# Activations of 32 of the 384 dense tokens from gathered rows of u

## The chip, the cores and the metric

The kernel runs on one core of a Trainium2 chip. The metric is the time of one execution on the device in microseconds, the median of several runs; lower is better. The core's engines run their own instruction streams in order: PE (matmul; its weight loads are listed apart as PEld), DVE (elementwise on vectors), ACT (activation functions and copies), POOL (here it only issues gathers), SP (it issues the plain DMAs). They wait for each other through semaphores.

## The reference

One transformer layer on 512 tokens of width 1024: a token-mixing part (sparse attention and a pooling mixer), and then a channel-mixing part, PEER: each token picks 128 of 16384 one-neuron experts.

```python
def peer_ffn(h, w_q, sub_keys, u, v):
    ...
        q = (hx @ w_q).reshape(TOKEN_BLOCK, PEER_HEADS, 2, PEER_HALF)
        s = jnp.einsum('nhpd,hpkd->nhpk', q, sub_keys).astype(jnp.float32)
        top_s, top_i = lax.top_k(s, PEER_TOPK)
        ...
        expert = (i1 * N_KEYS + i2).reshape(TOKEN_BLOCK, PEER_HEADS * PEER_TOPK)
        gate = jax.nn.softmax(best_s, axis=-1).reshape(TOKEN_BLOCK, PEER_HEADS * PEER_TOPK).astype(hx.dtype)
        u_sel = u[expert]
        v_sel = v[expert]
        act = jax.nn.gelu(jnp.einsum('nd,ned->ne', hx, u_sel), approximate=False)
        return jnp.einsum('ne,ned->nd', gate * act, v_sel)
```

u and v are tables of 16384 rows of 1024 float32 (4 KB a row, 64 MB a table). A token needs 128 rows of each.

## The kernel before

The token mixing takes the first part of the program and is not touched. The channel mixing treats the 512 tokens in two ways.

**Dense tokens** (384, `ND`): the activation of every one of the 16384 experts is computed for every dense token, whether the token picked it or not, and a gate matrix that is zero for all experts not picked removes the rest. The experts are cut into 128 chunks of 128. For a chunk, `fetch` loads 512 KB of the transposed u (tile `ue`), ACT rounds it to a float32r high part (`uhe`), DVE subtracts to get the low part (`ule`), and PE forms the product with h2 (also split in high and low) in 24 matmuls, 8 slices of k times 3 passes, each 384 columns wide, into a PSUM tile `pse`; ACT applies gelu. Later the chunk is multiplied by its gates (`gated`), split again (`weights`: `Wh`, `Wl` from the weights, `vh`, `vl` from 512 KB of v), and contracted with v in 18 matmuls of 512 columns (`contract`, tiles `acc`).

**Sparse tokens** (the last 128): `sparse` gathers the 128 picked rows of u, one for each of the 128 tokens in an indirect DMA (512 KB), and DVE takes the dot product of each row with the token's h2 (`hx`) in one instruction with an accumulator (line 756); then the same for v (line 767), where each row is scaled and added to `sacc`.

The program has two stages in the channel mixing. **The act stage**: PE computes the activations of the first chunks (`dense_acts`, 59 of them) while the product keys are selected (`ProductKeys`, on DVE) and the gate matrix is built (`gates`): DVE makes one-hot matrices (`on`, `oa`) for 4 tokens at a time, PE multiplies them (tiles `gm`), ACT copies the result to `st`, SP writes it to DRAM (`gd`). Of the 59 chunks 35 stay in SBUF (`KEPT = HOLD - 1`), the other 24 (`SPILL`) are written to DRAM (`ad`). How the two kinds of work interleave follows from `act_until` with the shares in `FILL`; outside the last stage the order on an engine is then made by a scheduler. **The last stage** goes through the 128 chunks in an order written by hand: in iteration c it prepares the weights of chunk c+1, multiplies chunk c+2 by its gates, issues some rows of `sparse` (`EARLY`, `RATE` or `late` rows for an iteration), for c < 24 reloads a spilled chunk, for the next 69 iterations computes the activations of one more chunk (`multiply`), and contracts chunk c. So there are 24 iterations with reloads, 69 with activations, and 35 (`KEPT`) with the contraction alone. The tiles `v`, `vh`, `vl`, `Wh`, `Wl` have two buffers, rows five, the gates of eight chunks (`g`) two.

Of the kernel before, what the change touches and what calls it, by code (L numbers as in the profile page):

```python
# [20 lines left out]
P = 128  # L21
# [13 lines left out]
ND = DENSE * P  # L35
NEXP = 128
GT = 16
GJ = 8
HOLD = 36
SPILL = 24  # L40
# [3 lines left out]
EARLY = 0.8  # L44
DELAY = 2.0
RATE = 3.0
# [6 lines left out]
FILL = (0.36, 0.72, 1.0)  # L53
# [11 lines left out]
K_ID, K_IOTA, K_BLK, K_RC, NCONST = 0, 128, 256, 384, 448  # L65
# [5 lines left out]
def layer(ctx, tc, xT, cvec, w_ada, cols, consts, w_in, w_grp, w_up, w_out, w_pq, subk, u, uT, v, out):  # L71
# [14 lines left out]
    ad = tc.dram_tile([SPILL, P, ND], F32, name="ad")  # L86
# [8 lines left out]
    with ExitStack() as pre:  # L95
# [405 lines left out]
        hx = k2.tile([P, D], F32, name="hx")  # L501
# [74 lines left out]
    def dense_acts(n):  # L576


        for c in range(n):
# [19 lines left out]
    with ExitStack() as win:  # L599
# [38 lines left out]

# [435 lines left out]
```

## Time and profile before

| | |
|---|---|
| time before, median of 3 runs | 1548.25 us (1547.19 to 1548.95) |
| the profiled execution | 1546.26 us, span of its instructions 1544.5 us |
| PE busy | 1501.2 us, 97% of the span, 8011 matmuls |
| PE weight loads | 1308.0 us, 85% |
| DVE busy | 1282.3 us, 83% |
| ACT busy | 650.7 us, 42% |
| POOL busy | 324.6 us, 21% |
| DMA | 394.69 MB, 256 GB/s over the span |

The act stage lies between about 397 and 725 us, the last stage between 725 and 1544 us. A matmul's busy time is counted from its start to its modelled end, and matmuls are pipelined, so that the next one starts well before that end: durations of matmuls must not be added; what PE can do is read from the distance between the starts of neighbouring matmuls. The same holds, by some 0.1 us, for DVE.

### The profile page before, as it was taken

Reading aid. Unit: us, or ns where it says so; the run is one execution under the profiler, and the core shown is the slowest. Engines: PE = TensorE matmul, PEld = TensorE weight load, DVE = VectorE, ACT = ScalarE, POOL = GpSimd, SP = SyncE. Lnnn points to the kernel's source line nnn. Section 1 sums busy time; section 2 is a strip of 40 time slices with the busy share of each in tenths; the row PEclk is TensorE's granted clock in tenths of the full one; section 3 lists DMA queues with packets and bytes.
Section 4 is the critical chain, followed back from the end, with each engine's and each line's share of the span. In section 5 each row is a group of like instructions: output and inputs, shape, how many; then the busy total and the mean of one; then the engine's idle time right before and its main releaser. Section 6 shows DMA issues by size and latency. Waiting matters only on the chain.

```text
span 1544.5 us, 22464 instructions
## 1 busy us (share of the span) xinstructions
PE 1501.2 (97%) x8011; PEld 1308.0 (85%) x8011; DVE 1282.3 (83%) x2632; ACT 650.7 (42%) x1005; POOL 324.6 (21%) x318
## 2 busy tenths in 40 slices
PE   5999999999999999999999999999999999999998
PEld 3678788877899989899878999999999999998886
DVE  8799886866898898983778888888888888888887
ACT  4643555642345454554333333333333333333332
POOL 0000000000000000001123444444444444453320
PEclk9999999999999999999999999999999999999999
DMA  8422664531135656789889999999998999998983
GB/s 317 159 83 75 232 229 144 190 140 55 50 125 182 204 178 200 219 258 332 305 311 361 349 324 362 318 356 340 338 357 320 359 325 353 352 334 308 329 305 144
DMA packets 159121, 394.69 MB, mean 256 GB/s; under 512 B 13601, under 2 KB 69025, under 8 KB 158882
## 3 DMA queue, kind: packets, MB, share of 16 engines
q1 hardware_dynamic: 122146, 259.04, 48.0%
q0 software_dynamic: 36864, 134.23, 24.6%
q8 instruction: 62, 1.02, 0.3%
q14 instruction: 49, 0.40, 0.1%
HBM read 359.14 MB, written 34.08 MB: 255 GB/s over the span
## 4 chain that ended last, share of the span: by engine, by line
PE 76%; DVE 15%; DMA 5%; ACT 3%; issue 2%; SPq 0%; ACTq 0%; DVEq 0%
PE acc L829 28%; PE pse L570 6%; PE pse L569 6%; PE pse L568 6%; PE pse L585 4%; PE pse L587 4%; PE pse L586 4%; DMA v<-v 3%; PE gm L687 2%; DVE bias L348 2%; DVE ule L548 1%; DVE m L347 1%; PE po L471 1%; PE pso L172 1%; PE pso L173 1%
## 5 line engine op out<-in xcount | busy, mean ns | idle before, releaser
L754 POOL DMA_INDIRECT ur<-u,ei x128 | 156.8, 1225 | 630.5 <-ACT Wh L818 383.7
L829 PE MATMUL acc<-vl,Wh 128*128 128x512 f32 x768 | 237.1, 389 | 0.7 <-DVE vl L821 0.5
L829 PE MATMUL acc<-vh,Wh 128*128 128x512 f32 x768 | 236.8, 389 | 0.6 <-ACT vh L819 0.6
L829 PE MATMUL acc<-vh,Wl 128*128 128x512 f32 x768 | 237.4, 390 | 0.0
L762 POOL DMA_INDIRECT vr<-v,ei x128 | 164.9, 1288 | 208.3 <-DVE sacc L767 178.2
L821 DVE TENSOR_TENSOR vl<-v,vh 128x1024 fp32r<-128x1024 f32 x128 | 156.9, 1225 | 60.1 <-ACT vh L819 59.7
L570 PE MATMUL pse<-h2h,ule 128*128 128x384 f32 x552 | 185.2, 336 | 0.4 <-DVE ule L548 0.4
L569 PE MATMUL pse<-h2l,uhe 128*128 128x384 f32 x552 | 184.7, 335 | 0.0
L568 PE MATMUL pse<-h2h,uhe 128*128 128x384 f32 x552 | 184.4, 334 | 0.0
L548 DVE TENSOR_TENSOR ule<-ue,uhe 128x1024 fp32r<-128x1024 f32 x128 | 156.0, 1218 | 26.3 <-ACT uhe L547 26.1
L818 ACT ACTIVATE Wh<-gelu 128x384 fp32r<-128x384 f32 x104 | 54.6, 525 | 281.6 <-PE acc L829 169.5
L829 PEld LDWEIGHTS acc<-vl,Wh 128*128 128x128 f32 x768 | 143.9, 188 | 31.5 <-DVE vl L821 1.7
L585 PE MATMUL pse<-h2h,uhe 128*128 128x384 f32 x472 | 169.1, 358 | 1.0 <-ACT uhe L547 0.8
L829 PEld LDWEIGHTS acc<-vh,Wl 128*128 128x128 f32 x768 | 144.2, 188 | 30.0
L767 DVE SCALAR_TENSOR_TENSOR sacc<-vr,wt,sacc 128x1024 f32<-128x1024 f32 x127 | 162.9, 1282 | 2.8 <-DMA vr<-v,ei 0.4
L829 PEld LDWEIGHTS acc<-vh,Wh 128*128 128x128 f32 x768 | 143.1, 188 | 25.5 <-ACT vh L819 1.0
L587 PE MATMUL pse<-h2h,ule 128*128 128x384 f32 x472 | 160.1, 339 | 3.2 <-DVE ule L548 3.1
L586 PE MATMUL pse<-h2l,uhe 128*128 128x384 f32 x472 | 159.5, 338 | 0.0
L547 ACT ACTIVATE uhe<-ue 128x1024 fp32r<-128x1024 f32 x128 | 134.3, 1049 | 55.2 <-PE pse L586 45.9
L756 DVE SCALAR_TENSOR_TENSOR ur<-ur,hx 128x1024 f32<-128x1024 f32 x128 | 150.6, 1220 | 0.0
L819 ACT ACTIVATE vh<-v 128x1024 fp32r<-128x1024 f32 x128 | 135.8, 1061 | 12.2 <-DMA v<-v 12.2
L569 PEld LDWEIGHTS pse<-h2l,uhe 128*128 128x128 f32 x552 | 103.6, 188 | 3.2
(430 smaller groups left out, 2674.6 us busy)
## 6 DMA issues: line engine op xcount, KB each, us to landing
ue<-uT SPq DMA_DIRECT2D x128, 512.0 KB, 5.3
v<-v SPq DMA_DIRECT2D x128, 512.0 KB, 5.8
wada<-w_ada SPq DMA_DIRECT2D x48, 512.0 KB, 4.4
gd<-st SPq DMA_DIRECT2D x24, 1024.0 KB, 5.7
g<-gd SPq DMA_DIRECT2D x48, 512.0 KB, 7.8
ad<-gelu SPq DMA_DIRECT2D x24, 192.0 KB, 3.2
wgp<-w_in SPq DMA_DIRECT2D x8, 512.0 KB, 3.2
wga<-w_in SPq DMA_DIRECT2D x8, 512.0 KB, 5.0
```

The costliest lines, as they stand in the source:

```text
L548: V.tensor_tensor(lo, src, hi.bitcast(F32), op=ALU.subtract)
L568: T.matmul(p, hi[:, k, :], h2h[:, k, :n], start=(k == 0), stop=False)
L569: T.matmul(p, hi[:, k, :], h2l[:, k, :n], start=False, stop=False)
L570: T.matmul(p, lo[:, k, :], h2h[:, k, :n], start=False, stop=(k == DT - 1))
L585: T.matmul(ps, hi[:, k, :], h2h[:, k, :ND], start=(k == 0), stop=False)
L586: T.matmul(ps, hi[:, k, :], h2l[:, k, :ND], start=False, stop=False)
L587: T.matmul(ps, lo[:, k, :], h2h[:, k, :ND], start=False, stop=(k == DT - 1))
L754: G.indirect_dma_start(out=ur, out_offset=None, in_=u, in_offset=bass.IndirectOffsetOnAxis(ap=ei3[:, k:k + 1], axis=0))
L762: G.indirect_dma_start(out=vr, out_offset=None, in_=v, in_offset=bass.IndirectOffsetOnAxis(ap=ei3[:, k:k + 1], axis=0))
L767: V.scalar_tensor_tensor(sacc, vr, wt[:, k:k + 1], sacc, op0=ALU.mult, op1=ALU.add)
L821: V.tensor_tensor(vl, vr, vh.bitcast(F32), op=ALU.subtract)
L829: T.matmul(acc[tb][i], x[:, t], y[:, i * 512:(i + 1) * 512], start=(c == 0 and n == 0), stop=(c == NEXP - 1 and n == 2))
```

## The change

32 of the dense tokens (the first ones, `US`) no longer take part in the dense activations: `h2h[:, k, US:ND]` makes each of the 24 matmuls of a chunk 352 columns wide (3072 of them in all). Their 32 x 128 picked rows of u are gathered (`gathers`) in 32 indirect DMAs of 128 rows, 32 tokens times 4 groups of experts on the 128 partitions, into three row buffers; DVE forms the dot products, two rows behind the gathers. The generator is advanced by 0.4 of a row for each step of gate building in the three blocks of tokens. When all are done, `values` applies gelu, brings the results into the layout of the gates, multiplies them by the gates and builds the weight matrix of the 32 tokens with three bfloat16 parts, in place of the gates alone with two float16 parts. In the last stage these 32 columns are weights already: `gated` leaves them out, and `weights` takes them from the gate tile `gts` in instructions of their own.

Row buffers and tiles need SBUF: `HOLD` goes from 36 to 29 (28 chunks kept), `SPILL` from 24 to 38. So the act stage has 28 + 38 = 66 chunks instead of 59, and the last stage 38 iterations with reloads, 62 with activations and 28 with the contraction alone. `EARLY` is 1.0 instead of 0.8, `RATE` 2.95 instead of 3.0; `late` follows as (256 + 2 - 38 - 2.95 x 62) / 21 = 1.77 rows for an iteration, where it was (256 + 2 - 19.2 - 207) / 28 = 1.14.

```diff
+US = 32
+NU = ND - US
+UG = P // US
+UBUFS = 3
...
-HOLD = 36
-SPILL = 24
+HOLD = 29
+SPILL = 38
...
-EARLY = 0.8
+EARLY = 1.0
 DELAY = 2.0
-RATE = 3.0
+RATE = 2.95
...
-FILL = (0.36, 0.72, 1.0)
+SEGS = [(0, US, P, 0.30, 0.4), (1, 0, P, 0.64, 0.4), (2, 0, P, 0.93, 0.4), (0, 0, US, 1.0, 0.0)]
...
-            ps = pact.tile([P, S], F32, tag="act", name=f"pse{c}")[:, :ND]
+            ps = pact.tile([P, S], F32, tag="act", name=f"pse{c}")[:, :NU]
             for k in range(DT):
-                T.matmul(ps, hi[:, k, :], h2h[:, k, :ND], start=(k == 0), stop=False)
...
+                T.matmul(ps, hi[:, k, :], h2h[:, k, US:ND], start=(k == 0), stop=False)
...
+        def values():
...
+            zero = oh.tile([P, P], F32, tag="gs", name="uz", bufs=1)
+            V.memset(zero, 0.0)
+            for i in range(UG):
+                r = slice(i * US, (i + 1) * US)
+                A.activation(zero[r, r], uact[r], AF.Gelu)
+            ps = ptr.tile([P, 4, P], F32, tag="tr", name="uw")[:, 0, :US]
+            T.matmul(ps, zero, con[:, K_SEL:K_SEL + US], start=True, stop=True)
+            V.tensor_tensor(ugate, ps, ugate, op=ALU.mult)
+            part = oh.tile([P, 3, US], BF16, tag="part", name="upart", bufs=1)
+            for i in range(3):
+                A.copy(part[:, i, :], ugate)
+                if i < 2:
+                    V.tensor_tensor(ugate, ugate, part[:, i, :], op=ALU.subtract)
+            yield from build(0, 0, US, ukeys[:, 0, :], ukeys[:, 1, :], ulow, [part[:, i, :] for i in range(3)], BF16, 1.0)
...
+        def gathers():
+            x = tokens(0, US, "u")
+            e = oh.tile([P, P], F32, tag="gs", name="ue", bufs=1)[:, :US]
+            V.scalar_tensor_tensor(e, sel[0][0][:, :US], 128.0, sel[0][1][:, :US], op0=ALU.mult, op1=ALU.add)
...
+            for k in range(US + UBUFS - 1):
+                if k < US:
+                    rows.append(us.tile([P, D], F32, tag="row", name=f"uu{k}", bufs=UBUFS))
+                    G.indirect_dma_start(out=rows[k], out_offset=None, in_=u,
+                                         in_offset=bass.IndirectOffsetOnAxis(ap=uei[:, k:k + 1], axis=0))
+                i = k - UBUFS + 1
+                if i >= 0:
+                    V.scalar_tensor_tensor(rows[i], rows[i], 1.0, x, op0=ALU.mult, op1=ALU.mult, accum_out=uact[:, i:i + 1])
+                yield
...
+            for n, _ in enumerate(gates(tb, t0, t1) if i < DENSE else values()):
...
+                due += rate
+                while due >= 1:
+                    next(early, None)
+                    due -= 1
                 act_until(LEAD * DT + int(between * (f0 + (f1 - f0) * (n + 1) / steps)))
...
-        V.tensor_tensor(wv, wv, gts[n][:, :, e, :], op=ALU.mult)
+        V.tensor_tensor(wv, wv, gts[n][:, US // GT:, e, :], op=ALU.mult)
...
-        A.activation(wh, w, AF.Copy)
+        first = gts[c // GJ][:, :US // GT, c % GJ, :]
+        groups = lambda x: x[:, :US].rearrange("p (g t) -> p g t", t=GT)
+        A.activation(groups(wh), first, AF.Copy)
+        A.activation(wh[:, US:], w, AF.Copy)
         A.activation(vh, vr, AF.Copy)
-        V.tensor_tensor(wl, w, wh.bitcast(F32), op=ALU.subtract)
+        V.tensor_tensor(groups(wl), first, groups(wh).bitcast(F32), op=ALU.subtract)
+        V.tensor_tensor(wl[:, US:], w, wh[:, US:].bitcast(F32), op=ALU.subtract)
```

The order on DVE in the middle of the act stage, where the gates of the second block of tokens are built; before (`on` and `oa` are the one-hot matrices, `ule` the low part of a chunk of u, `ge`, `pra`, `prb` the key selection):

```order
L674 TENSOR_TENSOR on_1_40_5636<-irep,sel_1_4144 128x1024
L680 TENSOR_TENSOR oa_1_40_5638<-gt_1_2_5573,rest_2_5569 128x1024
L680 TENSOR_TENSOR oa_1_40_5640<-gt_1_2_5575,rest_2_5569 128x1024
L987 TENSOR_TENSOR ge_5821<-at_5819,pk_begin 128x2048
L663 TENSOR_TENSOR rest_4_5866<-irep,low_5276 128x512
L989 TENSOR_TENSOR pra_5823<-ge_5821,stp_5816 128x2048
L665 TENSOR_TENSOR ten_4_5868<-tens,keys_5286 128x256
L993 TENSOR_TENSOR prb_5949<-ge_5821,pk_step 128x2048
L548 TENSOR_TENSOR ule_5556<-ue_5554,uhe_5555 128x1024
L674 TENSOR_TENSOR on_1_48_5707<-irep,sel_1_4144 128x1024
L548 TENSOR_TENSOR ule_5625<-ue_5623,uhe_5624 128x1024
L680 TENSOR_TENSOR oa_1_48_5709<-gt_1_2_5573,rest_2_5569 128x1024
```

And the same place now (line numbers are those of the changed kernel; `uu` is a gathered row, `uact` its dot products, `best`, `pos`, `cand` the key selection):

```order
L786 SCALAR_TENSOR_TENSOR uu_5344,uact<-uu_5344,hxu 128x1024
L705 TENSOR_TENSOR on_1_40_5593<-irep,sel_1_4156 128x1024
L552 TENSOR_TENSOR ule_5509<-ue_5507,uhe_5508 128x1024
L711 TENSOR_TENSOR oa_1_40_5595<-gt_1_2_5526,rest_2_5522 128x1024
L711 TENSOR_TENSOR oa_1_40_5597<-gt_1_2_5528,rest_2_5522 128x1024
L1050 MAX best_5411<-cand_5305 128x8 x2
L1051 MAX_INDEX pos_5412<-best_5411,cand_5305 128x8 x2
L1052 MATCH_REPLACE cand_5305<-best_5411,cand_5305 128x50 x2
L1053 MAX best_5411<-cand_5305 128x8 x2
L1054 MAX_INDEX pos_5412<-best_5411,cand_5305 128x8 x2
L786 SCALAR_TENSOR_TENSOR uu_5423,uact<-uu_5423,hxu 128x1024
L705 TENSOR_TENSOR on_1_48_5671<-irep,sel_1_4156 128x1024
```

Each stretch of gate building has got a row's dot product beside it, and the key selection of the next block of tokens stands later against the gates than it did.

The order of SP's DMAs at the end of the act stage, before, from the last write of gates (`gd<-st`) on (`g<-gd` are the first loads of the last stage, `ad` the spilled activations):

```order
L690 DMA gd<-st_7_7372 128x16x128
L596 DMA ad<-gelu_7504 128x384
L557 DMA ue_7594<-uT 128x1024
L797 DMA g_7753<-gd 128x1024 x2
L596 DMA ad<-gelu_7557 128x384
L557 DMA ue_7628<-uT 128x1024
L797 DMA g_7753<-gd 128x1024
L596 DMA ad<-gelu_7591 128x384
L816 DMA v_7758<-v 128x1024
L557 DMA ue_7662<-uT 128x1024
```

Now, where the last write is that of the 32 tokens' weights (`st_1`):

```order
L721 DMA gd<-st_1_7815 128x16x128
L597 DMA ad<-gelu_7990 128x352
L558 DMA ue_8061<-uT 128x1024
L875 DMA g_8187<-gd 128x1024
L597 DMA ad<-gelu_8024 128x352
L875 DMA g_8187<-gd 128x1024
L558 DMA ue_8095<-uT 128x1024
L597 DMA ad<-gelu_8058 128x352
L875 DMA g_8187<-gd 128x1024
L897 DMA v_8192<-v 128x1024
```

After the last write of gates there were three more loads of u (`ue`), now there are two: the write stands nearer to the end of the act stage than it did, and the first load of gates as close behind it as before.

DVE in the iterations with the contraction alone, where an iteration has two rows of v; before:

```order
L805 TENSOR_TENSOR gelu_12117<-gelu_12117,g_13588 128x384
L767 SCALAR_TENSOR_TENSOR sacc<-vr_13953,wt,sacc 128x1024
L767 SCALAR_TENSOR_TENSOR sacc<-vr_13956,wt,sacc 128x1024
L820 TENSOR_TENSOR Wl_13981<-gelu_12117,Wh_13980 128x384
L821 TENSOR_TENSOR vl_13979<-v_13977,vh_13978 128x1024
```

And now:

```order
L883 TENSOR_TENSOR gelu_12777<-gelu_12777,g_13788 128x352
L845 SCALAR_TENSOR_TENSOR sacc<-vr_14411,wt,sacc 128x1024
L845 SCALAR_TENSOR_TENSOR sacc<-vr_14414,wt,sacc 128x1024
L904 TENSOR_TENSOR Wl_14439<-g_13788,Wh_14438 128x32
L905 TENSOR_TENSOR Wl_14439<-gelu_12777,Wh_14438 128x352
L906 TENSOR_TENSOR vl_14437<-v_14435,vh_14436 128x1024
```

The low part of the weights takes two instructions instead of one, and iterations with two rows are now the rule there (1.77 rows on average against 1.14).

## Rows read from the trace of the kernel before

**Rows 1.** Busy time in stretches: start and length, PE, PEld, DVE, ACT, POOL, clock, DMA

```profile
core 0: us, PE busy (x) PEld busy (x) DVE busy (x) ACT busy (x) POOL busy (x), PEclk, DMA share, GB/s
403.00:699.00 296.00, 287.03 (x2181) 267.95 (x2179) 270.47 (x927) 152.15 (x254) 0.00 (x0) 0.99 0.61 188
410.00:425.00 15.00, 12.28 (x60) 11.43 (x59) 15.00 (x100) 6.82 (x10) 0.00 (x0) 0.89 0.28 99
485.00:515.00 30.00, 30.00 (x250) 28.22 (x249) 21.80 (x62) 14.11 (x24) 0.00 (x0) 1.00 0.59 180
...
635.00:680.00 45.00, 45.00 (x368) 41.55 (x367) 44.93 (x132) 26.27 (x42) 0.00 (x0) 1.00 0.79 237
699.00:725.00 26.00, 26.00 (x152) 25.65 (x151) 11.24 (x13) 11.29 (x18) 5.50 (x5) 1.00 0.95 318
725.00:830.00 105.00, 103.35 (x458) 85.04 (x457) 74.64 (x108) 39.71 (x52) 17.31 (x18) 1.00 0.89 321
830.00:1391.00 561.00, 561.00 (x2854) 512.81 (x2854) 474.14 (x589) 200.33 (x272) 259.48 (x204) 1.00 0.94 344
```

**Rows 2.** The chain that ended last, from the act stage's end: start, length, what

```profile
572.40 0.47 PE gm L687 x8
...
724.81 19.96 PE acc L829 x88
...
829.75 4.09 PE acc L829 x18
838.01 4.09 PE acc L829 x18
```

**Rows 3.** PE in order of time, two places: start, length, instruction

```profile
187.07 0.28 PE L453 MATMUL lg<-k,qs 128*128 128x256 f32 x1
187.19 0.28 PE L452 MATMUL lg<-k,qs 128*128 128x256 f32 x1
...
1000.45 0.33 PE L568 MATMUL pse<-h2h,uhe 128*128 128x384 f32 x1
1000.63 0.33 PE L569 MATMUL pse<-h2l,uhe 128*128 128x384 f32 x1
```

**Rows 4.** DVE in order of time, iterations with activations

```profile
829.13 1.23 DVE L548 TENSOR_TENSOR ule<-ue,uhe 128x1024 fp32r<-128x1024 f32 x1 [0.32 <-ACT uhe L547]
830.27 1.22 DVE L756 SCALAR_TENSOR_TENSOR ur<-ur,hx 128x1024 f32<-128x1024 f32 x1
831.42 0.08 DVE L756 DVE_READ_ACCUMULATOR ur<-ur,hx 128x1 f32 x1
831.42 1.22 DVE L756 SCALAR_TENSOR_TENSOR ur<-ur,hx 128x1024 f32<-128x1024 f32 x1
```

**Rows 5.** Waits for v in the reload iterations: ACT and PE in order of time

```profile
794.11 1.06 ACT L819 ACTIVATE vh<-v 128x1024 fp32r<-128x1024 f32 x1 [3.37 <-DMA v<-v]
...
795.22 0.73 PE L829 MATMUL acc<-vh,Wh 128*128 128x512 f32 x2 [0.59 <-ACT vh L819]
```

**Rows 6.** DVE in order of time, iterations with the contraction alone

```profile
1417.10 1.23 DVE L821 TENSOR_TENSOR vl<-v,vh 128x1024 fp32r<-128x1024 f32 x1 [0.43 <-ACT vh L819]
...
1418.70 2.60 DVE L767 SCALAR_TENSOR_TENSOR sacc<-vr,wt,sacc 128x1024 f32<-128x1024 f32 x2
1421.22 0.55 DVE L820 TENSOR_TENSOR Wl<-gelu,Wh 128x384 fp32r<-128x384 f32 x1
1421.69 1.22 DVE L821 TENSOR_TENSOR vl<-v,vh 128x1024 fp32r<-128x1024 f32 x1
...
1424.49 0.56 DVE L820 TENSOR_TENSOR Wl<-gelu,Wh 128x384 fp32r<-128x384 f32 x1
```

**Rows 7.** Busy time in two stretches of heavy DMA, columns as in rows 1

```profile
830.00:900.00 70.00, 70.00 (x355) 63.66 (x355) 58.39 (x87) 24.41 (x34) 32.59 (x26) 1.00 0.97 360
1430.00:1450.00 20.00, 20.00 (x90) 16.54 (x89) 16.84 (x21) 7.57 (x10) 6.39 (x5) 1.00 0.96 364
```

**Rows 8.** DMA issues: kind and count, KB of one, median us to landing

```profile
v<-v SPq DMA_DIRECT2D x128, 512.0 KB, 5.8
...
gd<-st SPq DMA_DIRECT2D x24, 1024.0 KB, 5.7
g<-gd SPq DMA_DIRECT2D x48, 512.0 KB, 7.8
...
ur<-u,ei POOLq DMA_INDIRECT x128, 6.1
```

More of the change, by code (lines that the diff above doesn't have):

```diff
@@ L685, in gates @@
                             q, j = (t4 + k) // 2, k % 2
-                            for i in range(2):
-                                T.matmul(ps[:, k, :], two[:, q, :, j], gated[i][:, :, q, :, j], start=(i == 0), stop=(i == 1))
-                        A.activation(st[:, :, t8 + t4:t8 + t4 + 4], ps.rearrange("p k e -> p e k"), AF.Copy, scale=2.0 ** -SCALED)
+                            for i, x in enumerate(gated):
+                                T.matmul(ps[:, k, :], two[:, q, :, j], x[:, :, q, :, j], start=(i == 0), stop=(i == len(gated) - 1))
+                        A.activation(st[:, :, t8 + t4:t8 + t4 + 4], ps.rearrange("p k e -> p e k"), AF.Copy, scale=scale)
                         yield
@@ L714, in act_until, with tokens @@
                 done += 1
+        def tokens(t0, n, name):
+            hs = kt.tile([P, DT, P], F32, tag="pr", name=f"hs{name}", bufs=2)
+            shape = [P, DT, P // n, n]
+            V.tensor_tensor(hs.rearrange("p d (g t) -> p d g t", t=n),
+                            h2h[:, :, t0:t0 + n].bitcast(F32).unsqueeze(2).to_broadcast(shape),
+                            h2l[:, :, t0:t0 + n].bitcast(F32).unsqueeze(2).to_broadcast(shape), op=ALU.add)
+            rows = k2.tile([P, D], F32, tag="hx", name=f"hx{name}")
+            for j0 in range(0, DT, 4):
+                ps = ptr.tile([P, 4, P], F32, tag="tr", name=f"hxp{name}{j0}")
+                for j in range(4):
+                    T.transpose(ps[:, j, :], hs[:, j0 + j, :], ident)
+                A.copy(rows[:, j0 * P:(j0 + 4) * P].rearrange("p (j t) -> p j t", t=P), ps)
+            return rows
@@ L716, in layer @@
         for _ in select(0):
             act_until(done + DT)
+        early = gathers()
+        next(early)
         act_until(LEAD * DT)
-        steps = P // 4
         between = (KEPT + SPILL - LEAD - TRAIL) * DT
-        for tb in range(DENSE):
-            keys = coming(tb + 1)
-            for n, _ in enumerate(gates(tb)):
-                if n * KEYS[tb] // steps != (n + 1) * KEYS[tb] // steps:
+        f0, due = 0.0, 0.0
+        for i, (tb, t0, t1, f1, rate) in enumerate(SEGS):
+            keys = coming(tb + 1) if i < DENSE else iter(())
+            pace = KEYS[tb] if i < DENSE else 0
+            steps = (t1 - t0) // 4
+            if i == DENSE:
+                for _ in early:
+                    pass
+            for n, _ in enumerate(gates(tb, t0, t1) if i < DENSE else values()):
+                if n * pace // steps != (n + 1) * pace // steps:
```

107 lines of the change are left out of this document (62 added, 45 removed).

## The prediction

> **What bounds the kernel now.** I read first the busy time by stage. In the last stage PE is full: 561 of 561 us in the iterations with activations and 103.35 of 105 in those with reloads [rows 1]; the chain that ended last consists there of PE's blocks [rows 2]. In the act stage, 403 to 699 us, neither engine is full, PE 287.03 and DVE 270.47 of 296 us, but single stretches differ: at 410 to 425 DVE is full and PE is not, at 485 to 515 PE is full and DVE has 8.2 us of 30 free, at 635 to 680 both are full [rows 1]. So PE bounds that stage with DVE close behind. From 699 to 725 only PE's last chunks are left, and DVE is busy for 11.24 of 26 us [rows 1].
>
> **The price of a matmul.** Durations overlap, so I take the distance of starts: 0.12 us at 256 columns, 0.174 at 384 [rows 3]. The line through both gives 13.3 ns for 32 columns and 0.1605 us at 352. The chain agrees with 0.174: an iteration lasts 838.01 - 829.75 = 8.26 us, of which the 18 contractions are 4.09 and the 24 products the other 4.17 = 24 x 0.174 [rows 2]. The new price of a chunk is 24 x 0.1605 = 3.85 us. I exclude a floor above it, since 256 columns ran at 0.12.
>
> **The act stage.** A dot product costs DVE 1.145 us from start to start (830.27 to 831.42; reading the accumulator overlaps), a split `ule` 1.14 [rows 4]. DVE gets 32 x 1.145 = 36.6 us of dot products and, with 66 chunks in the stage instead of 59, seven more splits, 8.0: together 44.6 us up to the end of gate building. Its work of 270.5 becomes 315. PE, in the same stretch, saves 13.3 ns x 24 for each chunk, so it is no longer the one that is late: DVE's 25.5 idle us (296 - 270.5) are nearly used up. I leave 4 us of idle time, from bounds 0 (DVE never waits) and 15 (waits for gathers and for PE at the stage's start, as at 410, remain). That ends DVE's part at 403 + 315 + 4 = 722 instead of 699.
> Then PE has to finish. Before, that took 26 us. Now I count seven chunks, 27.0 us, and 96 gate matmuls `gm` at 0.47 / 8 = 0.0585 us [rows 2], 5.6: 32.6 us. The transfer behind the last gates is late next: a write of gates lands after 5.7 us and a load after 7.8 [rows 8], 13.5 us in sequence, and in SP's order only two loads of u, not three, are left to cover it. I take 2 us (0 to 4, a chunk's time). The last stage so begins at 722 + 32.6 + 2 = 756.5, not 724.8: **+31.7** (bounds +27, with no idle time and no wait on the gates, and +43).
> POOL issued nothing in this stage [rows 1], so its 32 gathers push nothing back. A gather lands 6.1 us after its issue [rows 8]; with three buffers it is issued two rows ahead of its dot product, about 2 x 10 us (320 us for 32 rows), so I cost the wait at nothing. `values` runs once, on 128 x 32 elements; I count it with the 4 us.
>
> **The last stage, PE.** Seven chunks fewer: -7 x 4.17 = **-29.2**. The 62 left: -62 x 24 x 13.3 ns = **-19.8**. In these iterations DMA has v (0.524 MB), u (0.524), an eighth of the gates (0.197) and 2.95 rows (1.547): 2.79 MB in 7.94 us, 351 GB/s. A stretch with 360 GB/s had PE full, 70 of 70 us [rows 7], so this costs nothing; if it did not hold, 2.79 MB at the 344 GB/s of the whole part [rows 1] would be 8.11 us, which I leave to the range.
>
> **Reload iterations.** One moved 0.524 + 0.197 + 0.8 x 0.524 + 0.197 = 1.337 MB in a contraction of 4.09 us [rows 2], 327 GB/s; now it is 0.524 + 0.197 + 0.524 + 0.180 = 1.425 MB, 348 GB/s, and there are 38 instead of 24. From 724.81 to 829.75 lie 25 contractions, 102.3 us, and 2.6 us of waiting; ACT waited 3.37 us for v there and PE 0.59 for ACT [rows 5]. Below: at the 360 GB/s of [rows 7] nothing is added. Above: at the 321 GB/s that this stretch moved [rows 1], 1.425 MB takes 4.44 us, 38 x 0.35 = 13.3, less the 2.6 already there: +11. 348 lies between the two, so I take the middle, **+6**.
>
> **Contraction alone.** Rows end seven iterations early, so 21 iterations hold 1.77 rows each. An iteration with two rows took DVE 4.59 us (1417.10 to 1421.69), one with a single row 2.80 to the last instruction and 0.47 for that, 3.27 [rows 6]. At 1.77 rows that is 3.27 + 0.77 x 1.32 = 4.29, 0.2 over PE's 4.09: 21 x 0.2 = 4, less some 2 that two buffers of lead give, +2. The second instruction for the low weights is hidden in narrower ones (one column in twelve of `Wl` and of `gated`; 0.08 us for a small instruction [rows 4]). DMA asks more: 0.524 + 0.197 + 0.928 = 1.649 MB, at the highest rate seen, 364 GB/s [rows 7], 4.53 us, 21 x 0.44 = 9.2; less some 3 for what was loaded ahead, **+6**. Bounds: +2 (DVE alone binds) and +22 (1.649 MB at 321 GB/s is 5.14 us, 21 x 1.05).
> The Trainium skill (HBM Reference, Specifications) gives about 425 GB/s for a core that streams alone. The highest stretch here shows 364; at the page's figure this term would be DVE's +2, and the sum four lower.
>
> **Sum.** 31.7 - 29.2 - 19.8 + 6 + 6 = **-5.3**. The profiled execution took 1546.26, so the changed one 1541.0; the median stood 1.99 above that execution, which gives **1543 us**.
>
> **Rivals.**
> - *The transfers stay hidden.* The reloads add nothing, the last iterations only DVE's 2, and DVE has no idle time in the act stage: 27 - 49 + 2 = -20, **1528 us**. For it: 360 and 364 GB/s at full PE [rows 7]. Against it: PE already waited for v at 327 GB/s [rows 5]. Chance 0.16.
> - *Slower: DMA does not keep up in the 4 us iterations.* If it sustains only the 321 GB/s of the reload stretch, at .89 of its share [rows 1], v comes late in 59 iterations: 31.7 - 49 + 11 + 22 = +15.7, **1564 us**. It decides from about 335 GB/s down. For it: the waits of [rows 5]. Against it: the rates of [rows 7] and that 321 was nearly all that was asked. Chance 0.22.
> - *Slower: the gathers come late.* DVE runs in order; a dot product whose row has not landed stops splits and one-hots behind it, and with them PE. Half a microsecond at each of 32 rows, 16 us, of which some 6 go into idle time that I have counted already: +10 on the forecast, **1553 us**. For it: the generator moves in steps of 0.4 row, so that rows bunch where gate steps are short. Against it: 6.1 us to landing against some 20. Chance 0.09.
> - *Slower: TensorE's clock falls while PE waits for DVE.* At 410 to 425, where DVE was full and PE idle for 2.7 us of 15, the granted clock was 0.89, so part of it was at 1.2 GHz [rows 1]; with DVE full at 635 to 680 it stayed 1.00, since PE had enough to do. In the new stage PE has about 5.3 us for a chunk of 3.85 (and gate matmuls). Were 20 chunks run at 1.2 GHz, each would take 7.7, 2.4 more than DVE: +48, **1591 us**. Chance 0.04. The Trainium skill (TensorE: Matmul & The Clock Gate, HAM oscillation) describes this: matmul bursts between waits that each start at the lower clock. The trace agrees with it at 410, and not at 635.
> - *The saving goes with the busy time of a matmul*, 0.33 us for 384 columns [rows 3]: 28 ns for 32 columns, 62 x 24 x 15 ns = 22 us more, and 7 x 24 x 15 ns = 2.5 at the act stage's end: **1518 us**. The starts speak against it. Chance 0.02.
>
> **How the numbers follow.** The forecast has 0.42, with a range of its own of 1537 to 1549; 0.05 is left for what I haven't thought of. The whole range, 1526 to 1566, holds the forecast, about two thirds of the hidden and of the DMA case (each centred 2 us inside an end) and the late gathers: 0.8. A measurement of this kernel can tell about 0.2%, 3 us, from no change, so "same" is 1545 to 1551. Faster: 0.28 of the forecast, the hidden case 0.16, the wide saving 0.02, unknown 0.02: 0.48. Same: 0.11 of the forecast, 0.03 and 0.01 of the transfers and gathers, 0.01 unknown: 0.16. Slower: 0.03 of the forecast, 0.19, 0.08, 0.04, 0.02: 0.36.
>
> **What would show it.** Starts of 352-column products 0.16 us apart and iterations with activations of 7.94 us. DVE's idle time in the act stage under 10 us, with DVE and not PE ahead of the chain there, and the last stage beginning at 750 to 762. Dot products that wait for the DMA would show the late gathers; a granted clock under 0.95 over the act stage the clock. Reload iterations of about 4.25 us with waits of ACT for v, contraction-only ones of about 4.4 with DMA above .95. I am wrong if the act stage keeps more than 20 us of DVE idle time, or if DMA stays at 320 GB/s with PE waiting for v throughout.

## The result, and the profile after

The changed kernel takes 1562.46 us (median of 4, 1561.36 to 1566.1) where the kernel before took 1547.72 (median of 4, 1544.28 to 1548.95): 1.0103 times as long, 95% interval 1.0079 to 1.0127. I had forecast 1543. The time lies in the range given, on the other side of no change. The profiled execution took 1566.1 us, span 1564.3, the longest of the four; e5 below gives a second trace.

From PE's rows in order of time I take four marks: the first contraction (the act stage ends), the first contraction behind a product of the last stage, the first one behind its last product, and PE's last instruction. Between the second and the third lie the periods of product and contraction (68 before, 61 after). The stretch of the reloads ahead of them holds 38 contractions (24 before) and the first block of products, which I count as one contraction more: 39 and 25. All times in us:

| kernel | act stage ends | reload iterations | of it beyond 4.09 for each | products and contractions | rest |
|---|---|---|---|---|---|
| before | 724.65 | 104.94 (25) | 2.7 | 561.68 (68 x 8.26) | 147.23 |
| after | 761.12 | 177.39 (39) | 17.9 | 495.72 (61 x 8.127) | 124.67 |
| after, e5 | 759.61 | 176.30 (39) | 16.8 | 495.72 | 124.57 |
| spills alone, e2 | 759.11 | 164.41 (39) | 4.9 | 503.86 (61 x 8.26) | 122.74 |

The windows of the changed kernel, columns as in [rows 1]:

```profile
403.00:699.00 296.00, 275.57 (x2078) 256.37 (x2077) 285.76 (x958) 142.53 (x243) 41.31 (x32) 0.99 0.74 237
699.00:725.00 26.00, 24.02 (x187) 22.72 (x185) 22.54 (x44) 14.83 (x27) 0.00 (x0) 0.93 0.65 212
761.00:939.00 178.00, 166.95 (x713) 134.12 (x712) 132.13 (x234) 66.53 (x120) 43.57 (x41) 0.98 0.91 323
939.00:1434.00 495.00, 495.00 (x2560) 449.05 (x2559) 427.31 (x578) 181.71 (x305) 229.45 (x179) 1.00 0.94 347
1434.00:1564.00 130.00, 122.15 (x525) 97.11 (x523) 118.13 (x164) 44.98 (x82) 57.84 (x36) 1.00 0.81 301
```

In the act stage DVE is now busy for 285.76 of 296 us, where it was 270.47, and PE for 275.57, where it was 287.03 [rows 1]: the two have changed places. PE is full in the iterations with products, as before. In the 178 us of the reloads PE is idle for 11, and its granted clock is 0.98.

The chain that ended last, in the last stage (start, length, what):

```profile
767.87 11.79 DMA v<-v
...
829.67 10.48 DMA v<-v
...
865.62 10.02 DMA v<-v
...
902.47 9.31 DMA v<-v
...
938.67 4.13 PE acc L914 x18
946.80 4.13 PE acc L914 x18
```

Against [rows 2]: a period is 946.80 - 938.67 = 8.13 us, not 7.94, and about every 36 us, which is eight iterations, a load of v of some 10 us stands in the chain.

Two waits of the act stage (403 to 737 us; who waited for whom, us in all, times, longest):

```profile
ACT uhe L551 <- DMA ue<-uT: 28.0, 11, 4.8
DVE ule L552 <- ACT uhe L551: 12.1, 10, 3.4
```

DVE no longer waits for PE there; most of its idle time it spends on a high part that ACT forms late, in part because u came late. The gathered rows made DVE wait for 0.4 us in all. DVE's last one-hot matrix of the gates ends at 735.66 us, where it ended at 689.41 before; up to there DVE is idle for 332.66 - 318.85 = 13.8 us:

```profile
403.00:735.66 332.66, 310.25 (x2373) 288.97 (x2371) 318.85 (x1016) 162.97 (x279) 41.31 (x32) 0.98 0.72 233
```

DVE in order of time, iterations with the contraction alone and two rows, answers [rows 6]:

```profile
1444.61 1.22 DVE L906 TENSOR_TENSOR vl<-v,vh 128x1024 fp32r<-128x1024 f32 x1
1446.18 2.60 DVE L845 SCALAR_TENSOR_TENSOR sacc<-vr,wt,sacc 128x1024 f32<-128x1024 f32 x2
1448.70 0.19 DVE L904 TENSOR_TENSOR Wl<-g,Wh 128x32 fp32r<-128x32 f32 x1
1448.80 0.52 DVE L905 TENSOR_TENSOR Wl<-gelu,Wh 128x352 fp32r<-128x352 f32 x1
1449.23 1.22 DVE L906 TENSOR_TENSOR vl<-v,vh 128x1024 fp32r<-128x1024 f32 x1
```

From `vl` to `vl` 4.62 us, which was 4.59: the small instruction costs next to nothing, as I had it.

### The profile page after: what moved, and what is told of

Same layout as the page of the kernel before. It is cut to its first block, busy times and chain, and to the rows that moved or that the text cites. A ratio compares the mean times of both kernels' runs of the same rounds, so it can differ in the third digit from the quotient of the medians.

```text
span 1564.3 us, 22996 instructions
## 1 busy us (share of the span) xinstructions
PE 1495.7 (96%) x8054; PEld 1288.9 (82%) x8054; DVE 1329.1 (85%) x2839; ACT 661.4 (42%) x1146; POOL 375.1 (24%) x350
## 3 DMA queue, kind: packets, MB, share of 16 engines
q8 instruction: 63, 1.03, 0.3%
## 4 chain that ended last, share of the span: by engine, by line
PE 67%; DVE 15%; DMA 10%; ACT 3%; issue 3%; POOL 1%; SPq 0%; ACTq 0%; DVEq 0%; POOLq 0%
PE acc L914 22%; PE pse L569 5%; PE pse L570 5%; PE pse L571 5%; DMA v<-v 4%; PE pse L588 3%; PE pse L586 3%; PE pse L587 3%; DMA vr<-v,ei 2%; DVE ule L552 2%; DMA ue<-uT 2%; PE gm L718 2%; DVE vl L906 2%; DVE oa L711 1%; DVE uu L786 1%
## 5 line engine op out<-in xcount | busy, mean ns | idle before, releaser
L914 PE MATMUL acc<-vl,Wh 128*128 128x512 f32 x768 | 241.2, 395 | 6.4 <-DVE vl L906 6.3
L914 PE MATMUL acc<-vh,Wh 128*128 128x512 f32 x768 | 239.9, 393 | 7.4 <-ACT vh L903 7.4
L914 PE MATMUL acc<-vh,Wl 128*128 128x512 f32 x768 | 239.4, 393 | 0.0
L832 POOL DMA_INDIRECT ur<-u,ei x128 | 151.9, 1187 | 339.7 <-DVE ur L834 150.8
L840 POOL DMA_INDIRECT vr<-v,ei x128 | 178.9, 1398 | 166.5 <-DVE sacc L845 127.5
L906 DVE TENSOR_TENSOR vl<-v,vh 128x1024 fp32r<-128x1024 f32 x128 | 156.8, 1225 | 68.7 <-ACT vh L903 68.5
L586 PE MATMUL pse<-h2h,uhe 128*128 128x352 f32 x528 | 179.9, 341 | 2.4 <-ACT uhe L551 1.7
L588 PE MATMUL pse<-h2h,ule 128*128 128x352 f32 x528 | 176.2, 334 | 6.1 <-DVE ule L552 5.8
L914 PEld LDWEIGHTS acc<-vl,Wh 128*128 128x128 f32 x768 | 143.4, 189 | 44.6 <-DVE vl L906 14.5
L587 PE MATMUL pse<-h2l,uhe 128*128 128x352 f32 x528 | 175.3, 332 | 0.0
L914 PEld LDWEIGHTS acc<-vh,Wh 128*128 128x128 f32 x768 | 142.6, 189 | 35.8 <-ACT vh L903 9.8
L914 PEld LDWEIGHTS acc<-vh,Wl 128*128 128x128 f32 x768 | 145.1, 189 | 31.2
L901 ACT ACTIVATE Wh<-g 128x32 fp32r<-128x32 f32 x128 | 29.3, 229 | 318.0 <-PE acc L914 310.4
L569 PE MATMUL pse<-h2h,uhe 128*128 128x352 f32 x496 | 162.4, 328 | 0.0
L570 PE MATMUL pse<-h2l,uhe 128*128 128x352 f32 x496 | 162.4, 327 | 0.0
L571 PE MATMUL pse<-h2h,ule 128*128 128x352 f32 x496 | 162.2, 327 | 0.0
L834 DVE SCALAR_TENSOR_TENSOR ur<-ur,hxs 128x1024 f32<-128x1024 f32 x128 | 151.7, 1219 | 0.3 <-DMA ur<-u,ei 0.3
L782 POOL DMA_INDIRECT uu<-u,uei x32 | 41.3, 1291 | 310.9 <-DVE uu L786 163.6
```

What stands on the lines that cost most here:

```text
L569: T.matmul(p, hi[:, k, :], h2h[:, k, t], start=(k == 0), stop=False)
L570: T.matmul(p, hi[:, k, :], h2l[:, k, t], start=False, stop=False)
L571: T.matmul(p, lo[:, k, :], h2h[:, k, t], start=False, stop=(k == DT - 1))
L586: T.matmul(ps, hi[:, k, :], h2h[:, k, US:ND], start=(k == 0), stop=False)
L587: T.matmul(ps, hi[:, k, :], h2l[:, k, US:ND], start=False, stop=False)
L588: T.matmul(ps, lo[:, k, :], h2h[:, k, US:ND], start=False, stop=(k == DT - 1))
```

## The experiments

The kernel before ran beside each, with medians of 1545.71 to 1547.23 us; the ratios are to those runs. e1 was run once, without a ratio.

**e1: what a product's matmul costs, by its columns**

```diff
+    WIDTHS = ((0, 384), (0, 352), (32, 384), (0, 320), (64, 384), (0, 256), (16, 368))
...
+            T.matmul(p[:, a:b], hi[:, k, :], h2l[:, k, a:b], start=False, stop=False)
```

> The kernel before, in whose last stage the products of a chunk take in turn the columns 0:384, 0:352, 32:384, 0:320, 64:384, 0:256 and 16:368 (the first and the last of the 24 matmuls stay 384 wide; the partial sums left out make the activations of the other columns wrong). Price of a matmul as the distance of starts. Theory 1, the prediction's line: 384 at 0.174, 352 at 0.160, 320 at 0.147, 256 at 0.12, wherever the columns start; seven chunks save 3.2 us, 69 chunks about 32, so about 1516 us. Theory 2, a price of its own for 352 columns (0.1667, as the changed kernel's trace shows): 0.1667 for all three ranges of 352, and 320 and 256 on the line. Theory 3, the first column matters: 0:352 at 0.160 and 32:384 at 0.1667. Theory 4, a floor of 0.1667 from the weight load: 320 and 256 cost 0.1667 too.

1517.42 us. PE in order of time; in either pair the second row is the 16th start behind the first, the first pair is of columns 0:352, the second of 32:384:

```profile
866.04 0.32 PE L574 MATMUL pse<-h2h,uhe 128*128 128x352 f32 x1
868.61 0.32 PE L575 MATMUL pse<-h2l,uhe 128*128 128x352 f32 x1
...
873.22 0.33 PE L575 MATMUL pse<-h2l,uhe 128*128 128x352 f32 x1
875.88 0.33 PE L577 MATMUL pse<-h2h,ule 128*128 128x352 f32 x1
```

16 steps in 2.57 and in 2.66 us: 0.1606 and 0.1663. All chunks of the last stage agree, in the mean: 256 columns 0.119, 320 from column 0 and from 64 0.146, 352 from column 0 0.161, from column 16 0.160, from column 32 0.1665, 384 0.174. The line holds to about a nanosecond; the range 32:384 alone lies 6 ns above it. Theory 3. In e1 the columns of the result move together with those of h2; in e6 and e11 those of h2 alone.

**e6 and e11: the same products from column 0**

```diff
-                T.matmul(ps, hi[:, k, :], h2h[:, k, US:ND], start=(k == 0), stop=False)
+                T.matmul(ps, hi[:, k, :], h2h[:, k, :NU], start=(k == 0), stop=False)
...
+BLOCKS = (2, 1, 0, 3)   # e11 only
```

> The changed kernel with its products over the columns 0:352 of h2 in place of 32:384 (the activations then belong to other tokens). Theory 1: the column at which the moving operand starts sets the price; in the last stage 0.160 instead of 0.1667, the iteration 7.96 instead of 8.13 us, 62 x 0.16 = 10 us less in the stage, and some us in the act stage: 1549 to 1553 us. Rival: 0.1667 is the phase between contraction and product in this program, wherever the columns start: no change, 1560 to 1564 us.

> The changed kernel with the 32 tokens taken from the end of the dense columns (352:384; the blocks of tokens are selected in the order 2, 1, 0), so that the products run over the columns 0:352; it computes the whole reference. Theory 1: the start column's price alone, as in e6: iterations with activations of 7.97 us instead of 8.13, 1550 to 1555 us. Rival: e6 was faster for another reason, its values; then 1559 to 1564 us.

1554.28 (ratio 1.0048, 1.0018 to 1.0078) and 1552.04 us (1.0052, 1.002 to 1.0083). The chain of e11:

```profile
942.64 4.10 PE acc L914 x18
950.61 4.10 PE acc L914 x18
```

Its period is 7.97 us, against 8.13, and both kernels spend 486.0 us where the change spends 495.72: 9.7 us, as expected. e11's time lies in its theory's range, e6's 1.3 us above it. The contractions became 0.03 us shorter too, although nothing in them was edited. The reload stage of e11 stayed as slow as that of the change (178.43 us).

**e2 and e8: the spills alone**

```diff
-HOLD = 36
-SPILL = 24
+HOLD = 29
+SPILL = 38        # e2, with EARLY = 1.0, RATE = 2.95;  e8: SPILL = 31
```

> The kernel before with HOLD 29, SPILL 38, EARLY 1.0 and RATE 2.95 alone: no gathered rows of u, products 384 wide. Theory 1: the spills are what costs most beside the dot products; PE's work only moves from the last stage to the act stage (7 chunks, 29 us), the reload iterations wait some 15 us more and the last iterations some 4, so 1562 to 1570 us. Theory 2, the prediction's terms: +6 and +6, 1558 us. Rival: the reloads wait only because the gathers and the 32 tokens' weights came late at the end of the act stage; then 1548 to 1552 us.

> The kernel before with HOLD 29 and SPILL 31, so that seven chunks more are written out and read back while the act stage keeps its 59 chunks (e2 had 66 and took 13.4 us more than before). Theory 1: the cost in e2 comes from the seven more chunks in the act stage, where they cost 34.5 us for 29.2 us of matmuls, and from the rows pressed into fewer iterations; spilling itself costs little: 1546 to 1550 us. Rival: each spilled chunk costs, in the act stage by its write and in the last stage by its read; then half or more of the 13.4 us stays, 1553 us or more.

e2 1559.08 us (1.0085, 1.0055 to 1.0114), e8 1547.0 (1.0014, 1.0001 to 1.0027). The spilling itself is almost free. What costs in e2 is the move of seven chunks: the act stage becomes 34.5 us longer for 29.2 us of matmuls (+5.3), the reloads wait 2.2 us more, and the rest, with 1.77 rows an iteration, loses 122.74 - (147.23 - 7 x 4.09) = 4.1. Together that is 11.6 us, against the 11.4 by which its profiled execution was longer. So its time is theory 2's, by other terms. e2 has the reload iterations and the rows of the changed kernel, more bytes in each (a spilled chunk is 32 columns wider), and 4.9 us of waits there where the change has 17 to 18: neither bytes nor their mean rate explain the change's waits.

**e3 and e15: dot products without, or rows without, in the act stage**

```diff
-                    V.scalar_tensor_tensor(rows[i], rows[i], 1.0, x, ..., accum_out=uact[:, i:i + 1])
+                    pass                                   # e3
-                    G.indirect_dma_start(out=rows[k], ...)
+                    V.memset(rows[k], 0.0)                 # e15: three times, no gather
```

> The changed kernel without its 32 dot products (the gathers stay; the 32 tokens' activations are wrong). Theory 1: DVE is what bounds the act stage, and with 36.6 us less on it PE bounds it again; the last stage begins at about 742 to 746 instead of 761, 15 to 19 us earlier, and the time is 1543 to 1548 us. Rival: the act stage is late because loads of u wait behind gathers, spills and gate writes; then it begins no more than 5 us earlier, 1557 us or more.

> The changed kernel without the 32 gathers: the dot products read three row buffers that are set to zero once (the 32 tokens' activations are wrong). Theory 1: DVE's instructions are what the rows cost in the act stage, not their transfers; the last stage begins within 2 us of where it began (759 to 761 us), 1558 to 1563 us. Rival: the gathers delay the loads of u, for which DVE waited 12 us through ACT; then it begins at 752 to 756 us, 1550 to 1557 us.

e3: 1551.47 us (1.004, 1.0024 to 1.0056), the act stage ends at 752.81, 8.3 us earlier. e15: 1554.19 (1.0059, 1.0041 to 1.0077), it ends at 748.26, 12.9 us earlier. In the seven traces whose act stage is that of the change it ends between 758.4 and 762.5, so both differences are clear, though not which of them is larger. e3 falls between its theories. In e15 the rival wins, with an act stage that ends 4 us earlier even than the rival had it: the transfers cost about as much as the instructions. e15 up to the end of its last one-hot matrix, and its waits up to there:

```profile
403.00:723.92 320.92, 306.25 (x2369) 286.12 (x2368) 317.48 (x1013) 163.16 (x279) 0.00 (x0) 0.99 0.61 189
DVE ule L552 <- ACT uhe L551: 1.7, 3, 1.1
ACT uhe L551 <- DMA ue<-uT: 7.3, 7, 2.2
```

ACT waits 7.3 us for u instead of 28.0, and DVE, with the same work, is idle for 3.4 us instead of 13.8. No run leaves out both, so the two differences are not to be added.

**e4, e5, e7: the waits of the reload stage**

```diff
+                if c >= SPILL:
+                    next(rows, None)       # e4
...
-EARLY = 1.0
+EARLY = 0.8                                # e7
-RATE = 2.95
+RATE = 3.15                                # e7
```

> The changed kernel without the 36 rows that fall into the 38 reload iterations (the first 36 of 128 experts of the sparse tokens are left out). Theory 1: v comes late there because the rows share the DMA with it; without them an iteration moves 0.90 MB, 220 GB/s, and the 18 us in which PE waits between 761 and 939 fall to 3 or less: 1546 to 1549 us. Rival: v is late because of its two buffers and the spills that stand before it on SP's queue; then 12 us or more of the waits stay, 1556 us or more.

> The changed kernel once more, nothing edited: a second trace beside that of the result, whose execution took 1566.1 us, the longest of its four. Theory 1: the 18 us of waiting in the 39 contractions of the reload stage belong to the change (what is added in an iteration, the 32 tokens' weights, delays v): 15 to 18 us again. Theory 2: they vary from execution to execution with the phase of the transfers; here 5 to 12 us, and the execution is 1558 to 1562 us.

> The changed kernel with EARLY 0.8 in place of 1.0 and RATE 3.15 in place of 2.95, so that the last iterations have 1.54 rows instead of 1.77. Theory 1: rows beside reloads and beside bare contractions make v late, and the middle has room for them: reloads 3 to 6 us less, last iterations 2 to 4 less, 1553 to 1558 us. Rival: the middle's DMA, 2.90 MB in 8.13 us or 357 GB/s, has no room; its iterations grow and take back what is won: 1560 us or more.

e4 1551.35 us (1.0035, 1.0015 to 1.0055): 163.88 us of reload iterations, 4.4 of waits. e5 1561.69 (1.01, 1.0053 to 1.0147): the waits come again, 16.8 us, theory 1. e7 1551.87 (1.0035, 1.002 to 1.0049): 171.40 us of reloads and 118.77 us in the rest, 5.9 less than the change; the iterations with products stayed at 8.127, so the middle had room for the rows. e4's waits are near its theory 1, its time lies between its theories; e7 came out 1 us below its own. e4 shows that rows are part of the lateness of v. With e2, which has the same rows, they aren't the whole.

**e9 and e10: what holds v up**

```diff
-        if e in (1, 3, 5) and n + 1 < NEXP // GJ:
-            gate_piece(n + 1, e // 2)
+        if e in (2, 4, 5) and n + 1 < NEXP // GJ:          # e9
+            gate_piece(n + 1, (2, 4, 5).index(e))
...
-        A.activation(groups(wh), first, AF.Copy)            # e10: vh ahead of Wh, vl ahead of Wl
```

> The changed kernel with the three loads of the next eight chunks' gates issued at chunks 2, 4 and 5 of an eight instead of 1, 3 and 5. Theory 1: the low weights of the 32 tokens now read the gate tile one iteration later than the last multiplication by gates did, so the first load of gates waits for them on SP's queue (5.7 us in four times) and comes in one lump with the second, and v behind it takes some 10 us; one chunk later it needn't wait: the waits of the reload stage fall from 14 to 18 us to 5 to 9, 1552 to 1557 us. Rival: what counts is only how much is moved in these iterations; the waits stay, 1559 to 1564 us.

> The changed kernel with the split of v (vh, vl) ahead of the split of the weights (Wh, Wl, in two instructions each now) on ACT and DVE. Theory 1: the two small instructions and the wider ones stand between the end of a contraction and the release of v's buffer; with v first its load starts 0.5 to 0.7 us earlier in each iteration, and half of the waits in the reload stage goes: 1552 to 1557 us. Rival: the weights are then what comes late, PE waits for Wh and Wl instead: 1559 to 1566 us.

e9 1567.25 us (1.0133, 1.0096 to 1.017), e10 1560.2 (1.0087, 1.0065 to 1.011). e10 shortened the reloads to 171.92 us, but not the whole by more than can be told; PE waited 5.2 us for `Wh`, as its rival had it. e9, with two runs, lies above both its ranges, and told nothing of its theory: SP's order in the last stage is the scheduler's, which put the gate loads back together: three of 512 KB left SP at 862.90, 864.17 and 867.28 us, with a load of v between them, though the code names them two iterations and one apart.

**e13: the order on SP kept as the code has it**

```diff
+            tc.keep_in_program_order(nc.sync.dma_start(out=gts[n][...], in_=gd[n, ...]))
+        tc.keep_in_program_order(nc.sync.dma_start(out=vr, in_=v[c * P:(c + 1) * P, :]))
+                tc.keep_in_program_order(nc.sync.dma_start(out=gelus[a], in_=ad[c]))
```

> The changed kernel with the loads of gates, of v and of the spilled activations kept on SP in the order in which the code names them, so that one load of gates goes out in every second iteration instead of three within two loads of v. Theory 1: v comes late because three gate loads, a row, a spilled chunk and v are under way together (409 GB/s, share 1.03 in the wait at 777 us); spread, the waits of the reload stage fall from 14 to 18 us to 4 to 8: 1550 to 1556 us. Rival: it is the mean load of the stage; the waits stay within 3 us of what they were, 1558 to 1564 us.

e13: 1560.1 us (1.0092, 1.0068 to 1.0115). Windows of the reload stage of e13, and of the changed kernel where v was waited for and behind that wait:

```profile
761.65:925.81 164.16, 161.91 (x709) 131.64 (x709) 129.88 (x232) 69.40 (x119) 45.57 (x41) 1.00 0.98 350
```

```profile
773.00:777.00 4.00, 3.54 (x16) 2.61 (x15) 3.34 (x6) 0.88 (x3) 0.74 (x1) 1.00 1.03 409
872.00:876.00 4.00, 3.36 (x15) 2.44 (x13) 0.10 (x1) 0.25 (x1) 0.46 (x1) 1.00 1.03 413
878.00:880.00 2.00, 1.88 (x5) 1.50 (x6) 2.00 (x6) 0.51 (x2) 0.09 (x1) 0.53 0.56 167
880.00:882.00 2.00, 2.00 (x7) 1.62 (x6) 1.10 (x2) 1.05 (x1) 0.99 (x1) 0.62 0.78 245
```

The stage falls from 177.39 to 164.16 us (39 x 4.09 = 159.5), with the same bytes at a higher mean rate, 350 GB/s instead of 323. In the change DMA ran at a share of 1.03, 409 to 413 GB/s, for the few us in which v was under way with the gate loads, a row and a spilled chunk. So the cause is the order on SP, not the mean. SP in the change, in e13 and in e2 (start, length, DMA):

```profile
863.45 0.32 SPq L875 DMA_DIRECT2D g<-gd  x1
863.97 0.49 SPq L946 DMA_DIRECT2D gelu52b<-ad  x1
864.51 0.42 SPq L875 DMA_DIRECT2D g<-gd  x1
865.62 0.33 SPq L897 DMA_DIRECT2D v<-v  x1
```

```profile
862.57 0.33 SPq L897 DMA_DIRECT2D v<-v  x1
862.95 0.44 SPq L875 DMA_DIRECT2D g<-gd  x1
863.44 0.43 SPq L946 DMA_DIRECT2D gelu53b<-ad  x1
867.94 0.33 SPq L897 DMA_DIRECT2D v<-v  x1
```

```profile
849.77 0.33 SPq L816 DMA_DIRECT2D v<-v  x1
850.23 0.34 SPq L797 DMA_DIRECT2D g<-gd  x1
852.23 0.43 SPq L797 DMA_DIRECT2D g<-gd  x1
854.05 0.33 SPq L816 DMA_DIRECT2D v<-v  x1
856.50 0.45 SPq L797 DMA_DIRECT2D g<-gd  x1
```

e13 changes two things: the gate loads go out singly, and a spilled chunk (`ad`) leaves behind v instead of ahead of it. e2 has the chunk ahead of v too and waits for only 4.9 us, so I take the lump of gate loads for the cause; no run separates the two.

e13's waits are theory 1's, but its time is the rival's, since the rest grew from 124.67 to 133.34 us. Most of that, 6.4 us, lies in two contractions near the end (7.97 and 6.62 us): the last four loads of v there stood on SP behind the writes of the sparse tokens' output, as in e14 below.

**e12, e14, e16: put together**

```diff
e12: columns 0:352 (e11), EARLY 0.8, RATE 3.15 (e7), gate loads as in e9
e14: columns and rates as in e12, SP's order as in e13
e16: as e14, with the order kept only up to chunk 38
```

> The three together: columns 0:352 as in e11, EARLY 0.8 and RATE 3.15 as in e7, gate loads at chunks 2, 4 and 5 as in e9. Theory 1: the gains are of different iterations and add up, 10 from the columns, 10 from the rates and some of the gates' beside them: 1537 to 1544 us, faster than before by 0.2 to 0.5%. Rival: shorter iterations with activations ask 2.90 MB in 7.97 us, 364 GB/s, and DMA takes back what the columns give: 1547 to 1552 us, no faster than before.

> The kernel of e12 with the gate loads at chunks 1, 3 and 5 as in the change, and the order on SP pinned as in e13. Theory 1: the lump of gate loads is what is left of the waits in the reload stage, which takes 162 to 166 us instead of 172: 1536 to 1541 us. Rival: the rates of e12 have already taken the waits away that the pinned order could take: 1543 to 1547 us.

> The kernel of e14 with the order on SP pinned for the loads up to chunk 38 alone, so that the last iterations have the scheduler's order again. Theory 1: in e14 the gate load that waits 10.6 us for the low weights holds up v in the last iterations (3.8 us of waits, a last part of 122.9 us where e12 had 118.9), and this goes: 1536 to 1540 us, 0.3 to 0.6% faster than before. Rival: what the last part gives was chance; 1541 to 1545 us, as e12 and e14.

e12 1544.5 us (0.9984, 0.9973 to 0.9995), e14 1541.16 (0.9974, 0.9954 to 0.9993), e16 **1533.19** (4 runs, 1530.45 to 1536.06; before 1547.23; 0.9903, 0.988 to 0.9926). e12 lies half a microsecond above its theory, e14 at the upper end of its own, e16 3 us below its own. SP near the end of e14, and what PE then waited for:

```profile
1487.18 0.33 SPq L863 DMA_DIRECT2D xr<-x2d  x1
1503.26 1.67 SPq L853 DMA_DIRECT2D out<-xr  x2
1505.02 1.82 SPq L897 DMA_DIRECT2D v<-v  x4
1509.84 0.73 PE L914 MATMUL acc<-vh,Wh 128*128 128x512 f32 x2 [2.86 <-ACT vh L903]
```

The writes (`out<-xr`) waited for DVE, and four loads of v behind them. Two contractions there took 7.10 and 5.02 us, all others ahead of them 4.08 or 4.09. So the wait that e16's theory names, 10.6 us of a gate load for the low weights, held up no contraction; e16 helped because it no longer pins v there, and v leaves ahead of the writes:

```profile
1494.02 12.76 SPq L899 DMA_DIRECT2D v<-v  x4
1508.22 1.68 SPq L853 DMA_DIRECT2D out<-xr  x2
```

e16 has both good parts: reloads 163.13 us, products 485.98, rest 118.95. Its windows of the reloads:

```profile
761.00:924.00 163.00, 161.12 (x709) 131.32 (x708) 122.43 (x213) 65.90 (x119) 35.54 (x33) 1.00 0.91 326
```

It beats both kernels and computes the whole reference; its act stage still ends at 760.65. Its median lies 8 us below e14's, of which the traces show only the 4 of the rest: e16's profiled execution was the slowest of its four, e14's (1534.96) the fastest of its six.

## Why the prediction was wrong

By its own steps, on the profiled executions (forecast -5.3, measured 1566.1 - 1546.26 = +19.8):

- **The price of a matmul failed, 11.6 us.** "The line through both gives 13.3 ns for 32 columns and 0.1605 us at 352" holds for columns 0:352 (0.161 in e1), and no floor stood above it. But the change multiplies columns 32:384, and there 352 columns cost 0.1667: the price also hangs on the column at which the moving operand starts. The step of -19.8 became 62 x (8.26 - 8.127) = -8.2. From start to start the products save 62 x (4.173 - 3.993) = 11.2, which is 7.5 ns for a matmul and not 13.3, and the contractions, 4.133 us instead of 4.087, take 2.9 back. e1, e6 and e11 settle that in the last stage the range of columns does it. Why column 32 costs and columns 0, 16 and 64 don't is open.
- **Reload iterations: the mechanism was half right, the size failed by 9 us.** Forecast +6 (0 to +11); measured 17.9 - 2.7 = +15.2, and +14.1 in e5. My bounds were mean rates of a stage. But v is loaded into two buffers, so that its load has some 6 us (an estimate: two contractions of 4.09, less 1.06 for `vh` and 1.22 for `vl`), and SP's queue sends three gate loads within two loads of v, which then take 8 to 12. e13 changes the order, and 13 us of waits go with it. Part of the 15 was a clock: in the windows at 878 and 880 us, behind PE's waits of 1.50 and 0.53 us for v, the granted clock was 0.53 and 0.62, mostly its lower level of 1.2 GHz, and pairs of contractions started 0.86 us apart instead of 0.45. A mean of 0.98 over the 178 us is worth some 3.6 us, by estimate.
- **Why e2 waits only 4.9 us is argued, not shown.** Its gate loads lie further apart: the second 2.0 us behind the first, where the change has 1.06. In e2 the first leaves right behind a load of v; in the change it first waits for the low weights of the 32 tokens, which read the gate tile an iteration later than `gated` did (SP waited 8.1 us for them in five times), a reader that I had overlooked in the diff. That wait isn't needed for the harm, nor enough: e13 keeps it (7.5 us) without harm, and e10 is free of it, has gate loads 0.9 us apart, and keeps 12.4 us of waits.
- **The act stage: +31.7 forecast, +36.5 and +35.0 measured**, inside the bounds, but in part by luck. That DVE takes PE's place was right. I had DVE done at 722 us and PE 34.6 us later; DVE was done at 735.7, and PE needed only 25.5 more, since six chunks and 20 gate matmuls were left then, not seven and 96. Most of DVE's 13.7 us is the term that I had put at nothing: "its 32 gathers push nothing back" failed. No dot product waited for its row (0.4 us), but the gathers made the loads of u late; DVE was idle for 13.8 us, and without the gathers for 3.4 (e15), where I had forecast 4.
- **The last iterations came out at their size**: +6 forecast, 124.67 - (147.23 - 28.6) = +6.0. DVE's period was as worked out, and PE's only wait there that the trace names is for DVE (`PE acc L914 <- DVE vl L906: 2.7, 7, 0.8`). But the +6 was the term of DMA, for which I had expected a share above .95; from 1434 to 1522 us it was 0.94, at 352 GB/s. Which of the two makes up the six is open.
- **The rivals.** The time came out beside that of the DMA rival (1564), not by its mechanism: DMA sustained 347 GB/s over the products and 350 in e13's reloads, and the last iterations cost 6, not 22. The late gathers had nearly their price (+10), by another way: u came late, not the rows. The Trainium skill (HBM Reference, Specifications) gives about 425 GB/s for a core alone; the trace now shows 413 in a short stretch, so the 364 of [rows 7] was not the limit. It was not the highest rate of the trace before either, as I had it: 818 to 848 us (below) moved 391. The clock rival did not come about in the act stage (0.99 over 403 to 699, and 0.93 from 699 to 725), but did in small after the waits for v. The Trainium skill (TensorE: Matmul & The Clock Gate, HAM oscillation) describes it as a matmul burst that starts slow after each wait for DMA; the trace agrees there, 0.53.

```profile
818.00:848.00 30.00, 29.59 (x148) 26.37 (x147) 26.63 (x38) 12.03 (x16) 10.83 (x10) 1.00 1.01 391
```

The measured terms sum to the measured change: 36.5 - 29.2 - 8.2 + 15.2 + 6.0 = +20.3, against +19.8.

## What to carry to other kernels

A price read from one shape holds for a slice only if the slice starts where that shape started; before a narrower operand is costed on a line, look whether its first column moves, and take the columns from the other end if it does. Where a double-buffered load feeds a stage, don't bound it by the mean rate: see which other transfers go out between two of its loads in the queue's real order, and whether a wait stands ahead of it there. Keeping SP's order was worth 13 us in one stage and cost 9 in the next, so it should be kept only where nothing that waits for its data, such as a write of results, then stands ahead of a load. And a transfer on another queue is not free because its own reader never waits: look for the loads that it makes late.

## What the runs showed of the hardware that I had not expected

In the last stage a matmul of 352 columns started 0.160 to 0.161 us after the one before it when its moving operand began at column 0 or 16, and 0.1667 when it began at column 32. But that is not the column alone: at the end of the act stage of e3, products of 32:384 ran at the lower price for the stretch below, 21 steps in 3.32 us, 0.158, where the changed kernel took 3.50 for the same number, 0.1667. The act stage of the changed kernel has such stretches too: 31 products from 628.8 us on at 0.158.

```profile
738.72 0.32 PE L587 MATMUL pse<-h2l,uhe 128*128 128x352 f32 x1
742.04 0.32 PE L587 MATMUL pse<-h2l,uhe 128*128 128x352 f32 x1
```

```profile
738.72 0.33 PE L586 MATMUL pse<-h2h,uhe 128*128 128x352 f32 x1
742.22 0.33 PE L586 MATMUL pse<-h2h,uhe 128*128 128x352 f32 x1
```

In the last stage it never did. What decides between the two is open.
